# Sixteen projection blocks as two Strassen groups of 512 + 512 columns

## The chip, the cores and the metric

The kernel runs on one core of a Trainium2 chip. The metric is the time of one execution in device microseconds; the median of several runs is given. All of the big products are float32 values split in two parts, a rounded high part ("hi") and the rest ("lo"), and each product is made as three TensorE matmuls: hi x hi, lo x hi and hi x lo.

## The reference

One encoder layer on x of 512 tokens by 2048:

```
h = rmsnorm(x, norm_g)
proj = h @ w_in                      # 2048 x 10752
qa, ka, va, za, qb, kb, vb, zb, ga, gb = split(proj)
oa = diff_attention(rope(qa), rope(ka), va)      # branch A: 8 heads, two softmaxes each
ob = gqa_attention(rope2d(rmsnorm(qb)), rope2d(rmsnorm(kb)), vb)   # branch B: 8 heads, 2 of k and v
ya = (rmsnorm(oa) * silu(za)) @ w_out_a
yb = (ob * silu(zb)) @ w_out_b
x = x + (sigmoid(ga) * ya + sigmoid(gb) * yb) @ w_o
return rmsnorm(x, final_g)
```

What matters here is proj. Its columns for q, k and v are numbered in 36 blocks of 128: 0 to 7 are A's k, 8 to 15 A's q, 16 to 23 A's v, 24 and 25 B's k, 26 and 27 B's v, and 28 to 35 B's q, one block for each of B's heads.

## The kernel before

**The order of the work.** First h is made, turned and split, while blocks 0, 1, 8 and 9 are computed plainly (`stream_steps`, L137). Then the four groups of `STRASSEN_BLOCKS` (L39), four blocks each, go through `strassen` (L186) by way of `project` (L429); then twelve more Strassen groups make the gates (L476 to L488). These sixteen groups follow each other on TensorE. Then come the sixteen heads in the order of `HEADS` (L41), with "fill" work between them, then w_out_a and, in four Strassen groups, w_o.

**A Strassen group** takes 512 columns as a left and a right half of 256, the 2048 rows of weights as an upper and a lower half, and the 512 tokens as two halves. Seven products of half the size (a11, a12, s1, s2, s4, s3, a22 by the names of their activation part) take the place of eight; the weight parts are combined by subtractions on VectorE (`sub`, L207, line L209) and the products by additions (`plus`, L239, line L240, and `done`). A product is 16 x 3 matmuls of 256 columns. Its weights come from HBM in two raw tiles of 128 x 1024 into eight slots (`raw_tile`, L110); `split_w` (L113) has ScalarE write w_hi (L103) and VectorE w_lo (L104) into the pool `wp` (L82, three buffers of each). Results are added up in a PSUM bank of the ring `acc`; `share_banks` (L67) says which of the eight banks are `acc` and which `aux`, and `bank` (L69) takes the next one. A finished quarter of a group is written to the DRAM tile pv by `keep_cols` (L299), one DMA for each block, issued on SP like all DMAs.

**Plain blocks.** `FILL_BLOCKS` (L40) are eight pairs of blocks that are computed plainly as fill work. Pairs with blocks under 16 go through `plain_rows` (matmuls of 512 columns), the others through `plain_cols` (L314; natural form, matmuls of 256 columns, x as the stationary part). A pair has eight steps, each a `yield` of `stream_steps`. Behind them stand 32 steps of w_out_b and one more. `fill(n)` (L817) makes n steps. The order of TensorE's instructions among the heads is the program's own (L822): six steps, a head's `turn`, two steps, then for every head `scores` 0 and 1, the last head's `finish`, f[0] steps, `scores` 2 and 3, the next head's `turn`, f[1] steps, `turn_p`, f[2] steps, with f the three digits of `FILLS` (L46).

**Pools.** Space in SBUF is given in stacked pools. Above xa lies xs (the tiles s1 to s4, 8 KB per partition for each of h and l, 64 KB in all), above that xn during the first stage (xt with 32 KB, and some 5 KB more), and sp (six tiles of 2 KB) after it. When xs and sp close, the pools at and atc of the heads take their place; the first tiles of atc are the tables ca, sa, tc and ts, loaded at L501 to L512. wp and the PSUM pool (L64) stay open from first to last. Elsewhere the scheduler orders each engine's instructions by the program and by what is ready.

## Time and profile before

| | us |
|---|---|
| median of 3 runs | 1378.22 (1376.71 to 1378.24) |
| the profiled execution's own time | 1376.67 |
| its span, first to last instruction | 1374.9 |
| TensorE, VectorE, ScalarE, GpSimd busy | 1350.2, 1081.1, 702.9, 84.5 |

The profile is of one execution. Busy time is the union of an engine's instructions; matmuls overlap in the record, so the time of one is read from start to start or from a count in a stretch, and not from its own duration. The sixteen Strassen groups lie between 69.4 and 714.5 us, the heads between 714.5 and some 1118 us.

### The profile page before, as it was taken

The numbers are of one execution on the slowest core, as the hardware profiler recorded it, in microseconds if no ns is written. First come the engines' busy times: TensorE is split into PE (matmuls) and PEld (weight loads), VectorE is DVE, ScalarE is ACT, GpSimd is POOL, SyncE is SP. The second block draws the span as 40 slices with busy tenths as digits, with TensorE's granted clock in tenths as the row PEclk, the third lists the DMA queues.
The fourth block names the chain that finished last, engine by engine and source line by source line (L and its number), as shares of the span: only waits on it lengthen the run. The fifth ranks groups of instructions, "written<-read, shape, count | busy, mean of one in ns | idle before, by whom it ended". The sixth has DMA issues, their size and how long they took to land.

```text
span 1374.9 us, 24100 instructions
## 1 busy us (share of the span) xinstructions
PE 1350.2 (98%) x9625; PEld 1274.1 (93%) x9625; DVE 1081.1 (79%) x1400; ACT 702.9 (51%) x1110; POOL 84.5 (6%) x94
## 2 busy tenths in 40 slices
PE   6999999999999999999999999999999999999997
PEld 6999999999999999999998888888788888899997
DVE  5977787777777777777759778787898858899886
ACT  7643333444444444444446675575676753354444
POOL 1000000000000000000003201000000010004322
PEclk9999999999999999999999999999999999999999
DMA  8245434543333444333377454545575446463333
GB/s 291 77 147 161 124 116 149 154 146 113 118 121 123 148 149 143 117 122 118 123 207 220 122 154 147 153 139 162 171 221 182 130 145 202 151 245 116 97 95 123
DMA packets 201743, 204.21 MB, mean 149 GB/s; under 512 B 11280, under 2 KB 175392, under 8 KB 200992
## 3 DMA queue, kind: packets, MB, share of 16 engines
q1 hardware_dynamic: 201632, 202.69, 47.5%
q8 instruction: 75, 1.23, 0.4%
q14 instruction: 36, 0.29, 0.1%
HBM read 165.68 MB, written 32.77 MB: 144 GB/s over the span
## 4 chain that ended last, share of the span: by engine, by line
PE 90%; DVE 4%; ACT 2%; DMA 1%; issue 1%; POOL 0%; SPq 0%; DVEq 0%; POOLq 0%; ACTq 0%
PE acc L234 55%; PE acc L175 27%; PE aux L621 3%; PE aux L608 2%; PE aux L739 1%; DVE w_lo L104 1%; PE aux L664 1%; PE aux L665 1%; DVE w_raw L209 1%; DMA rows<-og 1%; DMA xt<-in_x_dram 1%; PE aux L389 0%; DMA rows<-yg 0%; ACT sq L366 0%; ACT w_hi L103 0%
## 5 line engine op out<-in xcount | busy, mean ns | idle before, releaser
L103 ACT CAST w_hi<-w_raw 128x1024 fp32r<-128x1024 f32 x351 | 368.5, 1050 | 516.8 <-PE acc L234 397.9
L104 DVE TENSOR_TENSOR w_lo<-w_raw,w_hi 128x1024 fp32r<-128x1024 f32 x351 | 431.9, 1232 | 168.7 <-ACT w_hi L103 168.2
L209 DVE TENSOR_TENSOR w_raw<-w_raw 128x1024 f32<-128x1024 f32 x160 | 200.0, 1250 | 2.4
L234 PE MATMUL acc<-a2h,w_hi 128*128 128x256 f32 x384 | 108.7, 283 | 0.0
L234 PE MATMUL acc<-a2l,w_hi 128*128 128x256 f32 x384 | 108.7, 283 | 0.0
L234 PE MATMUL acc<-a2h,w_lo 128*128 128x256 f32 x384 | 108.7, 283 | 0.0
L234 PEld LDWEIGHTS acc<-a2h,w_hi 128*128 128x128 f32 x384 | 73.7, 192 | 0.0
L234 PEld LDWEIGHTS acc<-a2l,w_hi 128*128 128x128 f32 x384 | 73.7, 192 | 0.0
L234 PEld LDWEIGHTS acc<-a2h,w_lo 128*128 128x128 f32 x384 | 73.7, 192 | 0.0
L576 DVE TENSOR_REDUCE nmax<-aux 128x1 f32<-128x512 f32 x96 | 61.0, 681 | 7.5 <-PE aux L739 4.7
L175 PE MATMUL acc<-a1h,w_hi 128*128 128x512 f32 (+1 forms) x160 | 56.6, 358 | 0.2 <-ACT a1h L393 0.2
L175 PE MATMUL acc<-a1l,w_hi 128*128 128x512 f32 (+1 forms) x160 | 55.6, 353 | 0.1
L175 PE MATMUL acc<-a1h,w_lo 128*128 128x512 f32 (+1 forms) x160 | 55.7, 353 | 0.0
L175 PE MATMUL acc<-a2l,w_hi 128*128 128x512 f32 (+1 forms) x160 | 55.5, 348 | 0.0
L175 PE MATMUL acc<-a2h,w_hi 128*128 128x512 f32 (+1 forms) x160 | 55.5, 350 | 0.0
L175 PE MATMUL acc<-a2h,w_lo 128*128 128x512 f32 (+1 forms) x160 | 55.4, 347 | 0.0
L234 PE MATMUL acc<-s4h,w_lo 128*128 128x256 f32 x192 | 54.3, 283 | 0.0
L234 PE MATMUL acc<-a1h,w_hi 128*128 128x256 f32 x192 | 54.3, 283 | 0.0
L234 PE MATMUL acc<-a1l,w_hi 128*128 128x256 f32 x192 | 54.3, 283 | 0.0
L234 PE MATMUL acc<-a1h,w_lo 128*128 128x256 f32 x192 | 54.3, 283 | 0.0
L234 PE MATMUL acc<-s1h,w_hi 128*128 128x256 f32 x192 | 54.3, 283 | 0.0
L234 PE MATMUL acc<-s1l,w_hi 128*128 128x256 f32 x192 | 54.3, 283 | 0.0
(325 smaller groups left out, 4356.0 us busy)
## 6 DMA issues: line engine op xcount, KB each, us to landing
w_raw<-in_w_in_dram SPq DMA_DIRECT2D x136, 512.0 KB, 3.6
w_raw<-in_w_in_dram SPq DMA_DIRECT2D x64, 256.0 KB, 3.7
w_raw<-in_w_o_dram SPq DMA_DIRECT2D x32, 512.0 KB, 4.4
gg<-kept SPq DMA_DIRECT2D x32, 256.0 KB, 2.4
w_raw<-in_w_out_b_dram SPq DMA_DIRECT2D x32, 256.0 KB, 3.5
rows<-gg SPq DMA_DIRECT2D x32, 256.0 KB, 3.4
w_raw<-in_w_out_a_dram SPq DMA_DIRECT2D x32, 256.0 KB, 3.4
cols<-pv SPq DMA_DIRECT2D x26, 256.0 KB, 3.3
```

Of the source, the lines that this page charges most:

```text
L103: nc.scalar.copy(out=hi, in_=src)
L104: nc.vector.tensor_tensor(out=lo, in0=src, in1=hi.bitcast(F32), op=ALU.subtract)
L175: nc.tensor.matmul(out=acc[b][:, place], lhsT=l, rhs=r, start=first and kc == order[0] and k == 0 and i == 0, stop=last and kc == order[-1 ...
L209: nc.vector.tensor_tensor(out=d, in0=u, in1=v, op=ALU.subtract)
L234: nc.tensor.matmul(out=ps[u] if by_row else ps[:, u, :], lhsT=l, rhs=r, start=n % (2 if by_row else 4) == 0 and k == 0 and i == 0, stop=n ...
L576: nc.vector.tensor_reduce(out=nmax, in_=sps, axis=AX.X, op=ALU.max, negate=True)
L608: nc.tensor.transpose(out=tp[:, i * P:(i + 1) * P], in_=self.p[i][:, j * P:(j + 1) * P], identity=ident)
L621: nc.tensor.matmul(out=o, lhsT=l, rhs=r, start=j == 0 and i == 0, stop=j == NT - 1 and i == 2)
L664: nc.tensor.matmul(out=sp, lhsT=qs[:, sl], rhs=kh, start=True, stop=False)
L665: nc.tensor.matmul(out=sp, lhsT=qs[:, sl], rhs=kl, start=False, stop=True)
L739: nc.tensor.matmul(out=sp, lhsT=l, rhs=r, start=n == 0, stop=n == 2)
```

## The change

The first Strassen group stays. Blocks 20 to 35 become two groups of the new function `strassen_wide`: 512 left and 512 right columns, the same seven products, each with 8 x 2 x 3 matmuls of 512 columns. x is the stationary part, as in the narrow groups of the projection. A product adds up in a pair of PSUM banks; for that the PSUM pool is closed and opened again as four pairs, and after the wide groups as eight banks. The raw weights of a wide group are sixteen tiles, eight in the old slots and eight in a new pool `wide`, which opens when xn and the first parts pool have closed and also holds the sums u, c and t. The parts pool is closed and opened four times: three buffers of 128 x 1024 before, four of 128 x 512 for the wide groups (a split is now made for each 128 rows of weights), three of 128 x 1024 after. In the first wide group (`late`) the right upper part is loaded before the left lower one, and s1 is made before a12. The pairs (32, 33) and (34, 35) leave `FILL_BLOCKS`, so 81 steps stand between the heads instead of 97; `FILLS` and `HEADS` are new.

```diff
--- before.py
+++ after.py
@@ -36,14 +36,16 @@
     for i in range(n)
 }
 
-STRASSEN_BLOCKS = [(16, 17, 18, 19), (20, 21, 22, 23), (24, 25, 26, 27), (28, 29, 30, 31)]
-FILL_BLOCKS = [(32, 33), (2, 10), (3, 11), (34, 35), (4, 12), (5, 13), (6, 14), (7, 15)]
-HEADS = "B0 B1 A0 B2 B3 B4 B5 A1 A2 B6 B7 A3 A4 A5 A6 A7".split()
+STRASSEN_BLOCKS = [(16, 17, 18, 19)]
+WIDE_BLOCKS = [tuple(range(20, 28)), tuple(range(28, 36))]
+FILL_BLOCKS = [(2, 10), (3, 11), (4, 12), (5, 13), (6, 14), (7, 15)]
+HEADS = "B0 B1 A0 B2 B3 B4 B5 A1 B6 B7 A2 A3 A4 A5 A6 A7".split()
 
 WIDE = "0125"
 
 FILL_FIRST = 6
-FILLS = "141 141 131 131 030 021 032 142 121 350 121 131 332 331 222 232".split()
+FILLS = "131 121 131 121 030 021 022 131 130 120 131 131 222 222 222 122".split()
 
 
 @with_exitstack
@@ -61,8 +63,13 @@
     const = ctx.enter_context(tc.tile_pool(name="const", bufs=1))
     dram = ctx.enter_context(tc.tile_pool(name="dram", bufs=1, space=bass.MemoryType.DRAM))
 
-    ps_pool = ctx.enter_context(tc.tile_pool(name="ps", bufs=1, space=bass.MemoryType.PSUM))
+    ps_pools = ctx.enter_context(ExitStack())
     banks = {}
+    def new_banks(unit):
+        ps_pools.close()
+        banks["pool"] = unit, ps_pools.enter_context(
+            tc.tile_pool(name="ps_" + unit, bufs=1, space=bass.MemoryType.PSUM))
 
     def share_banks(**kw):
         banks.update(kw)
@@ -70,7 +77,8 @@
     def bank(kind, shape):
         ring = banks[kind]
         ring.append(ring.pop(0))
-        return ps_pool.tile([P, *shape], F32, name=kind, tag=f"bank{ring[-1]}")
+        unit, pool = banks["pool"]
+        return pool.tile([P, *shape], F32, name=kind, tag=f"{unit}{ring[-1]}")
 
     def acc_tile(*shape):
         return bank("acc", shape)
@@ -79,7 +87,11 @@
         return bank("aux", shape or (S,))
 
     wraw = ctx.enter_context(tc.tile_pool(name="wraw", bufs=1))
-    wp = ctx.enter_context(tc.tile_pool(name="wp", bufs=3))
+    wp = {}
+    def parts_pool(stack, bufs=3):
+        wp["pool"] = stack.enter_context(tc.tile_pool(name="wp", bufs=bufs))
 
     ident = const.tile([P, P], F32, name="ident")
     make_identity(nc, ident)
@@ -114,8 +126,7 @@
 
         shape = list(raw.shape)
         if free is None:
-            hi = wp.tile(shape, F32R, name="w_hi", tag="w_hi")
-            lo = wp.tile(shape, F32R, name="w_lo", tag="w_lo")
+            hi, lo = (wp["pool"].tile(shape, F32R, name=n, tag=n) for n in ("w_hi", "w_lo"))
         else:
             hi, lo = (raw_tile(free + i, shape[1:], F32R) for i in range(2))
         hi_lo(hi, lo, raw)
@@ -276,6 +287,83 @@
         o = [slots[2 * i:2 * i + 2] for i in range(4)]
         slots[:] = o[1] + o[0] + o[3] + o[2]
 
+    wide_slots = list(range(16))
+    def strassen_wide(w, left, right, act, wide, done, late=False):
+        H = NK // 2
+        def load(q, half, pieces):
+            tiles = []
+            for p in range(4):
+                n = wide_slots[q * 4 + p]
+                r = raw_tile(n, (2, S)) if n < 8 else wide.tile([P, 2, S], F32, name="w_raw", tag=f"w_wide{n}")
+                row, at = (half * H + p * 2) * P, 0
+                for c0, n in pieces:
+                    nc.sync.dma_start(out=r[:, :, at:at + n],
+                                      in_=w[row:row + 2 * P, c0:c0 + n].rearrange("(k p) n -> p k n", p=P))
+                    at += n
+                tiles.append(r)
+            return tiles
+        def sub(dst, x0, x1):
+            for d, u, v in zip(dst, x0, x1):
+                nc.vector.tensor_tensor(out=d, in0=u, in1=v, op=ALU.subtract)
+        def product(name, b):
+            ps = acc_tile(2, S)
+            ah, al = act[name]
+            for kk in range(H):
+                hi, lo = split_w(b[kk // 2][:, kk % 2, :])
+                for u in range(2):
+                    sl = slice(u * P, (u + 1) * P)
+                    for i, (l, r) in enumerate(((ah, hi), (al, hi), (ah, lo))):
+                        nc.tensor.matmul(out=ps[:, u, :], lhsT=l[:, kk, sl], rhs=r,
+                                         start=kk == 0 and i == 0, stop=kk == H - 1 and i == 2)
+            return ps
+        def tmp(tag):
+            return wide.tile([P, 2, S], F32, name="wide_" + tag, tag="wide_" + tag)
+        def plus(dst, ps, sb):
+            nc.vector.tensor_tensor(out=dst, in0=ps, in1=sb, op=ALU.add)
+            return dst
+        b11, b12 = load(0, 0, left), None
+        if late:
+            b12 = load(1, 0, right)
+        b21 = load(2, 1, left)
+        b12 = b12 or load(1, 0, right)
+        b22 = load(3, 1, right)
+        p1 = product("a11", b11)
+        u = tmp("u")
+        nc.scalar.copy(out=u, in_=p1)
+        if not late:
+            p2 = product("a12", b21)
+        sub(b11, b12, b11)
+        p5 = product("s1", b11)
+        if late:
+            p2 = product("a12", b21)
+        done(0, 0, plus(tmp("c"), p2, u))
+        sub(b11, b22, b11)
+        p6 = product("s2", b11)
+        plus(u, p6, u)
+        t = plus(tmp("t"), p5, u)
+        sub(b12, b22, b12)
+        p3 = product("s3", b12)
+        plus(u, p3, u)
+        done(1, 1, plus(tmp("c"), p5, u))
+        sub(b21, b21, b11)
+        done(0, 1, plus(t, product("s4", b22), t))
+        done(1, 0, plus(u, product("a22", b21), u))
+        o = [wide_slots[4 * i:4 * i + 4] for i in range(4)]
+        wide_slots[:] = o[0] + o[3] + o[1] + o[2]
     zg = dram.tile([2 * BW, S], F32, name="zg")
     gg = dram.tile([2 * D, S], F32, name="gg")
     og = dram.tile([2 * BW, S], F32, name="og")
@@ -335,8 +423,11 @@
 
         return stream_steps(w_in, column_pieces(blocks), NK, False, act, kept, **kw)
 
+    new_banks("bank")
     share_banks(acc=[0, 1, 2, 3], aux=[4, 5, 6, 7])
     with tc.tile_pool(name="xs", bufs=1) as xs:
+        phase = ExitStack()
+        parts_pool(phase)
 
 
         for n in ("s1", "s2", "s3"):
@@ -452,7 +543,29 @@
 
             project(STRASSEN_BLOCKS[0], early, in_xt, before={"s2": late_sums})
 
+        phase.close()
+        names = dict(enumerate(slots))
+        slots[:] = [names[i] for i in (2, 3, 0, 1, 4, 5, 6, 7)]
+        new_banks("pair")
+        share_banks(acc=[0, 1, 2, 3])
+        with tc.tile_pool(name="wide", bufs=1) as wide:
+            parts_pool(phase, 4)
+            for n, blocks in enumerate(WIDE_BLOCKS):
+                def kept(th, ch, v, blocks=blocks):
+                    keep_cols(blocks[ch * 4:ch * 4 + 4], th * 2, 2, v)
+                strassen_wide(w_in, column_pieces(blocks[:4]), column_pieces(blocks[4:]), xq, wide, kept, late=n == 0)
+            phase.close()
+        o = [wide_slots[4 * i:4 * i + 4] for i in (0, 2, 1, 3)]
+        order = [slots[n] for q in o for n in q if n < 8]
+        slots[:] = order[0:2] + order[4:6] + order[2:4] + order[6:8]
         with tc.tile_pool(name="sp", bufs=6) as sp:
+            parts_pool(phase)
+            new_banks("bank")
+            share_banks(acc=[0, 1, 2, 3], aux=[4, 5, 6, 7])
             def tmp():
                 return sp.tile([P, 2, 256], F32, name="kept", tag="kept")
 
@@ -487,7 +600,9 @@
 
                     strassen(w_in, c0 + g, c0 + g + 256, xq, False, tmp, gate)
 
+            phase.close()
+    parts_pool(ctx)
     share_banks(acc=[4, 5], aux=[6, 7, 0, 1, 2, 3])
 
 

```

## Rows read from the trace of the kernel before

**Rows 1.** The page: busy time by engine, and the span in 40 slices.

```profile
PE 1350.2 (98%) x9625; PEld 1274.1 (93%) x9625; DVE 1081.1 (79%) x1400; ACT 702.9 (51%) x1110; POOL 84.5 (6%) x94
PE   6999999999999999999999999999999999999997
DVE  5977787777777777777759778787898858899886
```

**Rows 2.** The chain that ended last: start us, us, what.

```profile
69.38 645.12 PE acc L234 x5376
...
731.81 1.05 ACT w_hi L103
732.86 0.75 issue
733.61 1.20 PE aux L587 x8
734.82 7.23 PE acc L175 x48
...
1019.89 8.17 PE acc L175 x36
...
1118.96 79.37 PE acc L175 x350
```

**Rows 3.** Busy time by stretch (us, instructions): a projection group, and the heads.

```profile
69.40:109.70 40.30, 40.30 (x338) 40.30 (x338) 29.55 (x28) 16.81 (x19) 0.00 (x0) 1.00 0.46 147
742.00:1118.00 376.00, 374.50 (x1880) 315.61 (x1879) 310.99 (x574) 254.91 (x524) 23.91 (x21) 1.00 0.54 162
```

**Rows 4.** TensorE by line and form: xcount | busy us, mean ns.

```profile
L175 PE MATMUL acc<-w_hi,a2h 128*128 128x256 f32 x64 | 19.0, 298 | 0.0
...
L175 PE MATMUL acc<-w_lo,a2h 128*128 128x256 f32 x64 | 18.8, 294 | 0.0
```

**Rows 5.** VectorE and ScalarE by line and form, same columns.

```profile
L104 DVE TENSOR_TENSOR w_lo<-w_raw,w_hi 128x1024 fp32r<-128x1024 f32 x351 | 431.9, 1232 | 168.7 <-ACT w_hi L103 168.2
L209 DVE TENSOR_TENSOR w_raw<-w_raw 128x1024 f32<-128x1024 f32 x160 | 200.0, 1250 | 2.4
L240 DVE TENSOR_TENSOR kept<-acc,kept 128x512 f32<-128x512 f32 x45 | 31.1, 691 | 21.4 <-PE acc L234 20.9
L104 DVE TENSOR_TENSOR kl<-kd,kh 128x512 fp32r<-128x512 f32 x16 | 10.9, 679 | 0.4 <-ACT kh L103 0.4
L802 DVE TENSOR_TENSOR rows<-acc,rows 128x512 f32<-128x512 f32 x16 | 10.8, 684 | 1.5 <-PE acc L175 1.4
L883 DVE TENSOR_TENSOR mg<-rows 128x512 f32<-128x512 f32 x16 | 10.5, 684 | 0.1
L103 ACT CAST w_hi<-w_raw 128x1024 fp32r<-128x1024 f32 x351 | 368.5, 1050 | 516.8 <-PE acc L234 397.9 <-PE acc L175 65.9 <-issue 44.5
L103 ACT CAST kh<-kd 128x512 fp32r<-128x512 f32 x16 | 9.9, 621 | 4.6 <-PE aux L739 3.3 <-PE aux L664 0.9
```

**Rows 6.** VectorE in order of time, 98 to 122 us: start us, us, what.

```profile
106.19 2.49 DVE L209 TENSOR_TENSOR w_raw<-w_raw 128x1024 f32<-128x1024 f32 x2
...
109.73 0.69 DVE L432 TENSOR_TENSOR xt<-acc,early 128x512 f32<-128x512 f32 x1
```

**Rows 7.** SP's DMA issues in order of time, 98 to 122 us, same columns.

```profile
99.66 0.88 SPq L303 DMA_DIRECT2D pv<-xt  x2
...
104.69 6.91 SPq L303 DMA_DIRECT2D pv<-xt  x4
113.48 0.35 SPq L501 DMA_DIRECT2D ca<-in_cos_a_dram  x1
```

**Rows 8.** DMA issues: xcount, KB each, median us to landing.

```profile
pv<-kept SPq DMA_DIRECT2D x24, 128.0 KB, 1.9
pv<-xt SPq DMA_DIRECT2D x8, 128.0 KB, 2.3
```

**Rows 9.** Stretches of 1 us: PEclk is the third column from the right.

```profile
734.00:735.00 1.00, 1.00 (x10) 0.95 (x9) 1.00 (x2) 0.58 (x2) 0.66 (x1) 0.88 1.06 315
735.00:736.00 1.00, 1.00 (x6) 1.00 (x6) 1.00 (x3) 0.49 (x2) 0.00 (x0) 0.50 0.99 259
...
738.00:739.00 1.00, 1.00 (x9) 1.00 (x9) 1.00 (x3) 0.00 (x0) 0.00 (x0) 0.92 0.55 168
```

**Rows 10.** Stretches between the transposes of heads A3 to A7.

```profile
1000.40:1028.10 27.70, 27.70 (x132) 23.15 (x131) 26.65 (x46) 20.11 (x39) 0.00 (x0) 1.00 0.75 222
1028.10:1058.40 30.30, 30.30 (x144) 25.30 (x143) 26.93 (x47) 21.93 (x42) 1.30 (x1) 1.00 0.59 187
1058.40:1081.10 22.70, 22.57 (x110) 18.73 (x108) 20.16 (x37) 17.65 (x37) 1.29 (x1) 1.00 0.44 138
1081.10:1108.80 27.70, 27.66 (x129) 23.05 (x130) 24.78 (x42) 19.28 (x38) 2.27 (x2) 1.00 0.45 145
```


## The prediction

> **What bounds the kernel now.** I read the page first: TensorE is busy for 98% of the span and in nearly every slice, VectorE for 79% [rows 1]. A busy TensorE can still wait, so the chain of waits in order of time came next [rows 2]. The reader is to see that it is almost TensorE alone. The sixteen Strassen groups of the projection and the gates are one piece of 5376 products in 645.12 us, so 120.0 ns for one of 256 columns, without a hole. In the heads a block of 36 products of 512 columns takes 8.17 us, so 227 ns each. The difference of 107 ns for 256 columns leaves about 13 ns for each product whatever its width: fewer, wider products are cheaper. Third came the stretches [rows 3]: in the heads VectorE is busy 311 of 376 us, a second engine close to its limit. So TensorE's issue rate bounds the kernel, and a change is worth what it takes from TensorE's list less every new hole in that list.
>
> **The products, a gain.** Three Strassen groups (blocks 20 to 31) go: 3 x 336 x 120.0 ns = 120.96 us. Two plain pairs (32,33 and 34,35) go from between the heads: six rows of 64 products of 256 columns, 384 x 120.0 ns = 46.08 us [rows 4, 2]; their form is natural, so they too are 256 wide. In come 2 groups x 7 products x 8 x 2 x 3 = 672 matmuls of 512 columns at 227 ns = 152.5 us. Net -14.5 us. That the trace never shows the new function makes the 227 ns a transfer: the 512-wide products of w_out run 350 in 79.37 us, the same 227 [rows 2], and load as many weights per product. I keep 225 to 230 ns (2 us either way).
>
> **VectorE and ScalarE inside a wide group, nothing.** A group needs 56 splits of 512 columns, 16 subtractions of 1024 and 7 additions of 1024. An addition that reads PSUM takes as long as one in SBUF (0.69 and 0.68 for 512), so by 0.68, 1.25 and 1.25 us [rows 5] that is 67 of 76.3 us at most, and less where instructions overlap (two subtractions in 2.49 us, [rows 6]). ScalarE has 56 x 0.62 + 1.1 = 36 us. TensorE covers both; without that cover a product boundary could cost one split, 0.7 us, 13 times.
>
> **First handover (group 16 to 19 to the wide ones), a loss.** The parts buffers w_hi and w_lo used to live for the whole kernel; now their pool is closed and opened again. In KB per partition above xs: old parts 24, then xn of 37; afterwards wide takes 8 x 4 + 3 x 4 = 44 and the new parts 16, so the new parts lie at 44 to 60, inside the old xn (24 to 61). What happens to such space is in the trace: ca, which depends on nothing in the projection, is loaded at 113.48 us, just when the last results written from xt (in xn) can have landed [rows 7]. So the first wide split starts at 113.48, where TensorE ran out of products at 69.38 + 40.32 = 109.70. Add ScalarE 0.62 and VectorE 0.68 for a split of 512, less two products that need only w_hi (0.45): 3.78 + 0.62 + 0.68 - 0.45 = 4.6 us, during which nothing else is ready. In the old kernel those splits were made two halves ahead. Bounds: 0 if the space is not waited for, 5.5 with a landing 0.9 us slower than the median of 1.9 to 2.3 us that such writes have [rows 8]. I take 4.6. The wide loads behind it (b21, b22) wait for the same space, but "late" puts s1 before a12, so they have two products (22 us) to land.
>
> **The ring of PSUM pairs in the first wide group, a loss.** With "late" the order is a11, s1, a12, s2, s3, s4, a22 on pairs 0, 1, 2, 3, 0, 1, 2. So s4 wants the pair of s1, and s1's sum is last read by the addition behind s3 (u + p3, then p5 + u). Those two additions of 1024 start when s3 ends: 1.14 + 1.25 + 0.1 for semaphores = 2.5 us in which TensorE waits; the splits of a22 wait behind those of s4, so nothing overtakes. The second group has the old order and meets no such reuse. No product boundary in the trace of before shows a wait of this kind [rows 2], so the lower bound is 0; the upper is 3.6, one more subtraction in between.
> The Trainium skill (Perfetto Trace Analysis, Matmuls) asks that independent matmul groups rotate through different PSUM banks so that evacuation lies beside the next group. By that rule this order is a fault; by the row alone the sum would be 4.2 us lower. The trace of before agrees with the rule only in that its rotation shows no wait.
>
> **Second handover (wide to gates), a loss.** The new parts pool (24 KB behind 12 KB of sp) lies inside wide's 44. Its first user waits for all of wide, so for the last result u of the last group: addition 1.25, then the delay from that addition's end to freed space, 113.48 - 110.42 = 3.06 us [rows 6, 7], with four result writes instead of two, 0.44 each, so 3.94. Then a full split, 1.05 + 1.23, less two products (0.24): 7.2 us. Bounds: 0 if only the tiles beneath are waited for (the parts would lie over weight tiles, which are free early), 8.5 with slow landings. I take 7.2, nearest to the first handover's row.
> The third handover (gates to heads) costs nothing: the last parts pool lies under xs, whose last reader s4 ends one product, 5.8 us, before the gates do, and a split needs 2.3.
> The tables (ca to ts_k) are issued on SP after the wide groups instead of at 113 us; SP's next urgent load comes only after a whole product, and the heads start some 480 us later.
>
> **The clock.** The one wait of TensorE in the middle of the kernel, from 731.8 to 733.6 us [rows 2], was followed by a granted clock of 0.50, the lower of the two levels, in 735 to 738 us; the missing shares add up to 0.12 + 3 x 0.50 + 0.08 = 1.7 us [rows 9]. The 48 products behind it took 7.23 us instead of 5.76. All three new holes are longer than this one, so 3 x 1.7 = 5.1 us. Bounds: 0, and 10 if the longer ones cost double.
>
> **The heads, a loss.** 16 of 97 steps go, the 46 us above. I follow the four stretches from A3 to A7 [rows 10]: 108.4 us, VectorE 98.5, with 27 steps (the digits of FILLS). After, 22 steps: each step is 12 products, 2.73 us of TensorE, but only half a split and half a product with gg, 0.62 + 0.34 = 0.96 us of VectorE [rows 5]. TensorE would need 108.4 - 13.7 = 94.7, VectorE 98.5 - 4.8 = 93.7: 99%, in a queue that works in order. The chain of softmax then surfaces; I take 1 us for each of four of these heads, 4 us. Bounds 0 (the slack is spread well) and 12 (2 us for each A head and the B heads before them). What is late next is turn_p, which waits for the last p.
>
> **Sum.** Against the profiled execution's own 1376.67 us: -14.5 + 4.6 + 2.5 + 7.2 + 5.1 + 4.0 = +8.9, so 1385.6; that execution is 1.55 us below the median of 1378.22, so I say 1386.
>
> **Rivals.**
> (a) Not slower: the parts buffers wait at neither handover, and TensorE's gain comes through. Place: the first split of each new pool; it decides if that split starts before the previous stage's last product ends. For it: the raw weight tiles are passed on in an order that has the first ones free early. Against: the row of ca. 1376.7 - 14.5 + 2.5 + 1.7 + 4 = 1370.4.
> (b) About the same: only the tiles beneath are waited for, so the first handover stays (xt is one tile) and the second goes, with its clock: 1385.6 - 7.2 - 1.7 = 1376.7. The row of ca fits this too.
> (c) VectorE becomes the bound of the heads: the term of 4 becomes 12 to 16, so 1394 to 1398. For it: the 99%. Against: VectorE's own durations overlap in part, so 99% overstates it.
> (d) The change does not shorten TensorE's list, if 512 columns cost twice 256: 672 x 240 = 161.3 instead of 152.5, so 1394. The rows of w_out speak against it.
>
> **How the numbers follow.** Forecast 0.54 (own range 1380 to 1394), a 0.20, b 0.12, c 0.12, d 0.02. 0.2% (2.8 us) is about what a measurement of this kernel can tell from no change, so the same means 1375.5 to 1381. Slower takes c, d and 0.48 of the forecast, 0.62; the same takes the forecast's other 0.06 and 0.10 of b, 0.16; faster takes a and the last 0.02 of b, 0.22. The range of 8 in 10 runs from 1370 to 1395.
>
> **What would show it.** In the changed kernel: 672 products on one new line at 227 ns; TensorE idle 4 to 5 us near 110 us, ended by ScalarE's first w_hi, which waited for a DMA; 2.5 us near 171 us, ended by an addition on VectorE; 7 us near 273 us; a clock of 0.5 after each. Gates untouched at 40.3 us a group; heads some 42 us shorter, not 46. I am wrong if the first w_hi of the new pools is ready before the stage before has ended, or if the heads shorten by the full 46.

## The result, and the profile after

The changed kernel takes 1399.63 us in the median of four runs (1398.56 to 1401.21), the kernel before 1377.47 in four (1375.69 to 1378.24): a ratio of 1.0164, with a 95% interval of 1.0146 to 1.0181. It is slower, as forecast, but by 22 us where 8 were forecast, and outside the range. The profiled execution took 1400.52 us, 0.9 above the median; its span is 1398.7 us, 23.8 more than before.

The page of the changed kernel, its busy times and TensorE's row of the 40 slices, answers to [rows 1]:

```profile
PE 1346.0 (96%) x8905; PEld 1238.6 (89%) x8905; DVE 1099.4 (79%) x1463; ACT 717.5 (51%) x1167; POOL 86.0 (6%) x94
PE   6998999899999999999999899999998999999997
```

TensorE has 720 instructions fewer, but only 4 us less of busy time, and four slices that were full are not. The stretches say where that lies (us, then TensorE, weight load, VectorE, ScalarE and GpSimd busy, granted clock, DMA share, GB/s). Before, the fifteen groups behind the first took 40.32 us each, 604.8 in all, without a hole [rows 2, 3]; then came the heads:

```profile
714.30:1118.80 404.50, 401.16 (x2084) 341.71 (x2083) 331.64 (x614) 269.16 (x563) 33.12 (x39) 1.00 0.55 164
```

Now the two wide groups and the first handover end at 281.7, the twelve gates at 768.2 and the heads at 1143.1:

```profile
109.80:114.50 4.70, 0.22 (x3) 0.03 (x1) 0.74 (x2) 0.70 (x2) 0.00 (x0) 0.78 0.20 58
114.50:281.70 167.20, 158.02 (x673) 129.65 (x673) 124.85 (x159) 71.57 (x115) 0.00 (x0) 0.96 0.41 126
119.50:171.00 51.50, 51.50 (x228) 42.62 (x228) 43.72 (x56) 24.51 (x39) 0.00 (x0) 1.00 0.45 143
...
281.70:768.20 486.50, 486.03 (x4032) 485.74 (x4033) 369.64 (x355) 212.71 (x232) 0.00 (x0) 1.00 0.44 135
768.20:1143.10 374.90, 358.24 (x1700) 296.23 (x1699) 315.46 (x605) 257.02 (x550) 33.99 (x39) 0.99 0.53 159
```

From 109.8 us on, wide groups and gates take 171.9 + 486.5 = 658.4 us, 53.6 more than the fifteen narrow groups. The heads take 374.9, 29.6 less than before. The rest of the kernel is unchanged (255.6 us against 256.1). 53.6 - 29.6 - 0.5 is 23.5, the difference of the spans within the reading of the borders.

The third of these rows tells that the products are as cheap as forecast: 228 matmuls of 512 columns in 51.5 us, 226 ns each, with TensorE busy throughout. So the list of TensorE did get shorter, by the 14.5 us of the forecast, and some 38 us went into waits and low clock. What TensorE waited for, in us in total, times and the longest (between 60 and 1150 us; those of over a us, and one of half a us that belongs to the second handover):

```profile
PE acc L186 <- DVE w_lo L116: 6.3, 1, 6.3
PE acc L245 <- ACT w_hi L115: 6.0, 1, 6.0
PE acc L324 <- ACT w_hi L115: 4.5, 1, 4.5
PE aux L702 <- DMA cols<-pv: 4.2, 1, 4.2
PE acc L324 <- DVE wide_c L332: 3.1, 1, 3.1
PE acc L186 <- DVE rows L917: 2.0, 1, 2.0
PE aux L723 <- DVE p L788: 1.9, 3, 1.0
...
PE acc L245 <- DVE w_lo L116: 0.5, 1, 0.5
```

L324 is the product of a wide group, L245 that of a narrow one, L186 a fill step between the heads. Three of these rows are the three forecast holes: L324 on w_hi (first handover), L324 on wide_c (the PSUM pair), L245 on w_hi (second handover, with the half us on w_lo right behind it). The timelines of SP, ScalarE and VectorE (start us, us, what) show each at its place:

```profile
110.75 1.16 SPq L391 DMA_DIRECT2D pv<-xt  x2
...
113.80 2.18 ACT L115 CAST w_hi<-w_raw 128x512 fp32r<-128x512 f32 x4 [11.48 <-DMA pv<-xt]
...
171.45 1.23 DVE L332 TENSOR_TENSOR wide_u<-acc,wide_u 128x1024 f32<-128x1024 f32 x1 [0.24 <-PE acc L324]
172.59 0.68 DVE L116 TENSOR_TENSOR w_lo<-w_raw,w_hi 128x512 fp32r<-128x512 f32 x1
173.18 1.22 DVE L332 TENSOR_TENSOR wide_c<-acc,wide_u 128x1024 f32<-128x1024 f32 x1
...
276.93 1.95 SPq L391 DMA_DIRECT2D pv<-wide_u  x4
...
280.58 2.94 ACT L115 CAST w_hi<-w_raw 128x1024 fp32r<-128x1024 f32 x3 [9.95 <-DMA pv<-wide_u]
```

At 113.8 us ScalarE splits the first wide tile and was released by the result writes from xt, as [rows 7] let one expect from ca. At 280.6 it was released by the writes from u, issued at 276.93, so 3.65 us earlier. Between them, at 171.45, stand the two additions that free the pair of s4, and between the two a split that the forecast had not seen in VectorE's queue. Behind each of the three holes the granted clock was 0.50, the lower level. The stretches in which TensorE worked at it, and two in the heads:

```profile
114.50:119.50 5.00, 5.00 (x12) 3.91 (x13) 5.00 (x7) 2.10 (x4) 0.00 (x0) 0.52 0.95 322
...
174.50:181.00 6.50, 6.45 (x16) 5.08 (x17) 1.39 (x2) 1.23 (x2) 0.00 (x0) 0.52 0.52 158
...
281.70:287.00 5.30, 4.83 (x22) 4.54 (x23) 3.68 (x4) 1.82 (x2) 0.00 (x0) 0.54 0.35 116
...
788.80:791.70 2.90, 2.83 (x11) 2.66 (x12) 2.90 (x7) 1.17 (x2) 1.12 (x1) 0.50 0.98 251
...
1085.00:1089.00 4.00, 4.00 (x10) 3.18 (x11) 2.82 (x3) 0.00 (x0) 0.00 (x0) 0.54 0.61 198
```

The missing shares of the first three add up to 2.4 + 3.1 + 2.4 = 7.9 us. With the waits of 4.5, 3.1, 6.0 and 0.5 us, that is 22.0 of the 53.6; the other 31.5 is the products' own longer list there (152.5 - 120.96). The last two stretches belong to the heads, whose waits are the other half of the story: in the list above those of L186, L702 and L723, with smaller ones (0.9 us on pl, 0.6 each on og1h and og1l), come to 16.5 us, against 3.2 before, of which the 1.8 at the start stands in [rows 2].

The heads A3 to A7 answer to [rows 10], between the same transposes; here the third of the four stretches, and all four together (us and the same columns):

```profile
1075.50:1109.70 34.20, 27.23 (x120) 22.11 (x119) 26.95 (x44) 19.95 (x41) 1.26 (x1) 0.90 0.47 146
...
1027.20:1132.70 105.50, 97.27 (x450) 80.03 (x448) 93.18 (x165) 74.90 (x152) 5.15 (x4) 0.97 0.50 153
```

VectorE has 93.2 us of work in them (93.7 forecast), but they take 105.5 us where the forecast had 94.7 + 4. The third stretch has most of the difference: TensorE stood there for 7 of 34.2 us. This is the wait of 6.3 us, in the timelines of ScalarE, VectorE and TensorE:

```profile
1076.38 1.03 ACT L115 CAST w_hi<-w_raw 128x1024 fp32r<-128x1024 f32 x1
...
1077.44 1.29 DVE L917 TENSOR_TENSOR rows<-acc,rows 128x512 f32<-128x512 f32 x2
...
1082.90 2.05 DVE L116 TENSOR_TENSOR w_lo<-w_raw,w_hi 128x1024 fp32r<-128x1024 f32 x1
...
1085.01 0.80 PE L186 MATMUL acc<-og1h,w_lo 128*128 128x512 f32 x1 [6.31 <-DVE w_lo L116]
```

The high part of the weights is ready at 1077.4. Its low part is made only from 1082.9 on: two products of rows (the fill steps' own), four pl and three y (the heads') stand before it in VectorE's queue, 5.5 us. A fill step that is there to cover the head waits mostly for the heads' own VectorE work.

### The profile page after: what moved, and what is told of

Its sections match the earlier page's. It is cut to its first block, busy times and chain, and to the rows that moved or that the text cites. A ratio compares the mean times of both kernels' runs of the same rounds, so it can differ in the third digit from the quotient of the medians.

```text
span 1398.7 us, 22873 instructions
## 1 busy us (share of the span) xinstructions
PE 1346.0 (96%) x8905; PEld 1238.6 (89%) x8905; DVE 1099.4 (79%) x1463; ACT 717.5 (51%) x1167; POOL 86.0 (6%) x94
## 5 line engine op out<-in xcount | busy, mean ns | idle before, releaser
L115 ACT CAST w_hi<-w_raw 128x1024 fp32r<-128x1024 f32 (+1 forms) x413 | 385.1, 934 | 531.4 <-PE acc L245 318.1
L116 DVE TENSOR_TENSOR w_lo<-w_raw,w_hi 128x1024 fp32r<-128x1024 f32 (+1 forms) x413 | 446.8, 1089 | 171.8 <-ACT w_hi L115 171.3
L220 DVE TENSOR_TENSOR w_raw<-w_raw 128x1024 f32<-128x1024 f32 x136 | 170.7, 1256 | 1.9
L245 PE MATMUL acc<-a2h,w_hi 128*128 128x256 f32 x384 | 108.7, 283 | 0.0
L245 PE MATMUL acc<-a2l,w_hi 128*128 128x256 f32 x384 | 108.7, 283 | 0.0
L245 PE MATMUL acc<-a2h,w_lo 128*128 128x256 f32 x384 | 108.7, 283 | 0.0
L245 PEld LDWEIGHTS acc<-a2h,w_hi 128*128 128x128 f32 x384 | 73.7, 192 | 0.0
L245 PEld LDWEIGHTS acc<-a2l,w_hi 128*128 128x128 f32 x384 | 73.7, 192 | 0.0
L245 PEld LDWEIGHTS acc<-a2h,w_lo 128*128 128x128 f32 x384 | 73.7, 192 | 0.0
L245 PE MATMUL acc<-a1h,w_hi 128*128 128x256 f32 x192 | 55.3, 288 | 6.0 <-ACT w_hi L115 6.0
L186 PE MATMUL acc<-og1h,w_lo 128*128 128x512 f32 x128 | 50.8, 396 | 6.3 <-DVE w_lo L116 6.3
L186 PE MATMUL acc<-a1h,w_hi 128*128 128x512 f32 (+1 forms) x160 | 56.3, 357 | 0.2 <-ACT a1h L484 0.2
L186 PE MATMUL acc<-a2h,w_hi 128*128 128x512 f32 (+1 forms) x160 | 56.1, 354 | 0.0
L245 PE MATMUL acc<-a1h,w_lo 128*128 128x256 f32 x192 | 55.3, 288 | 0.5 <-DVE w_lo L116 0.5
L186 PE MATMUL acc<-a2l,w_hi 128*128 128x512 f32 (+1 forms) x160 | 55.7, 349 | 0.0
L186 PE MATMUL acc<-a2h,w_lo 128*128 128x512 f32 (+1 forms) x160 | 55.7, 349 | 0.0
L186 PE MATMUL acc<-a1h,w_lo 128*128 128x512 f32 (+1 forms) x160 | 55.5, 351 | 0.0
L186 PE MATMUL acc<-a1l,w_hi 128*128 128x512 f32 (+1 forms) x160 | 55.2, 350 | 0.1
L245 PE MATMUL acc<-a1l,w_hi 128*128 128x256 f32 x192 | 55.1, 287 | 0.0
L245 PE MATMUL acc<-s1h,w_hi 128*128 128x256 f32 x192 | 54.3, 283 | 0.0
L245 PE MATMUL acc<-s1l,w_hi 128*128 128x256 f32 x192 | 54.3, 283 | 0.0
```

The costliest lines, as they stand in the source:

```text
L115: nc.scalar.copy(out=hi, in_=src)
L116: nc.vector.tensor_tensor(out=lo, in0=src, in1=hi.bitcast(F32), op=ALU.subtract)
L186: nc.tensor.matmul(out=acc[b][:, place], lhsT=l, rhs=r, start=first and kc == order[0] and k == 0 and i == 0, stop=last and kc == order[-1 ...
L220: nc.vector.tensor_tensor(out=d, in0=u, in1=v, op=ALU.subtract)
L245: nc.tensor.matmul(out=ps[u] if by_row else ps[:, u, :], lhsT=l, rhs=r, start=n % (2 if by_row else 4) == 0 and k == 0 and i == 0, stop=n ...
```

## The experiments

The kernel before, run beside each batch of them, had medians of 1375.1 to 1376.9 us, against 1377.5 beside the changed kernel. Ratios are to the kernel before of the same batch; a difference of medians from the changed kernel is good to some 2 us only, so the stages of the profiled executions stand beside it.

**The three holes one by one.** In e1_ring the two next pairs of the ring change places before s4 of the first wide group, so that s4 gets a pair that has been free for long.

```diff
+        if late:
+            r = banks["acc"]
+            r[0], r[1] = r[1], r[0]
         done(0, 1, plus(t, product("s4", b22), t))
```

> The first wide group takes its last two PSUM pairs in the other order, so that s4 gets the pair of a12 and a22 that of s1. Theory (TensorE waited for the pair of s1): the hole of 3.6 us near 171 us goes and the low clock behind it too (some 3.1 us), so about 6.7 us less than the changed kernel, near 1393 us. Rival (VectorE is simply behind at that boundary, with the splits of s4 late): a hole of 2 us or more stays near 171 us and the time falls by under 3 us.

Measured: 1394.58 us, 1.0142 of the kernel before (1.0120 to 1.0164), 5.0 less than the changed kernel by the medians and 6.2 by the spans. Its gates end at 762.2 us instead of 768.2, 6.0 earlier. Its list of TensorE's waits has the two handovers as they were and no row on wide_c:

```profile
PE acc L245 <- ACT w_hi L115: 6.0, 1, 6.0
PE acc L324 <- ACT w_hi L115: 4.5, 1, 4.5
```

So the order of products against the ring makes this hole, and its price is the wait (3.1 us) and the low clock behind it (3.1). The Trainium skill (Perfetto Trace Analysis, Matmuls) asks that independent groups rotate through different PSUM banks; the 6.0 us agree.

In e2_u_apart the sum u lies in a pool of its own, above the parts, so that what is written last from the wide groups is not in the space that the gates' parts take.

```diff
-            return wide.tile([P, 2, S], F32, name="wide_" + tag, tag="wide_" + tag)
+            return (up if tag == "u" else wide).tile([P, 2, S], F32, name="wide_" + tag, tag="wide_" + tag)
...
             parts_pool(phase, 4)
+            up = phase.enter_context(tc.tile_pool(name="up", bufs=1))
```

> The sum u lives in a pool of its own above the parts buffers, so that the space the gates' parts buffers come to lie in no longer waits for the last result's write to memory. Theory (the second handover waits for that write): the hole of 7 us near 275 us shrinks to the 1.3 us of the last addition (the PSUM pool is still handed over), without a low clock behind it: 7.0 + 2.4 - 1.3 = 8 us less than the changed kernel, near 1391.5 us. Rival (the PSUM handover or the first gate group's weights decide): a hole of over 4 us stays.

Measured: 1393.68 us, 1.0132 (1.0115 to 1.0149), 5.9 less. The wait of 6.0 us on w_hi is gone; what is late next is the addition itself:

```profile
PE acc L245 <- DVE wide_u L332: 1.7, 1, 1.7
```

So the second handover is the wait for u's result write, and rival (b), by which it costs nothing, falls; whether the space waits for the whole pool, or only because the new parts come to lie over u, this run does not tell. The gain is 2 us short of the 8 expected. In the profiled executions the gates end 7.7 us earlier (760.5 instead of 768.2), of which 1.5 is a shorter low clock behind the ring's hole (last section), and the heads, where nothing was changed, take 1.5 us longer.

In e3_parts_low the wide groups' parts pool is opened before `wide`, so it takes another part of the freed space, and closes after it.

```diff
+        parts_pool(phase, 4)
         with tc.tile_pool(name="wide", bufs=1) as wide:
-            parts_pool(phase, 4)
...
-            phase.close()
+        phase.close()
```

> The wide groups' parts pool opens before the pool wide, so it lies where the old parts were and no longer over xt. Theory (the first handover waits for the write of the last results out of xt): the hole of 5 us near 110 us shrinks to about 1 us, one split of 512, and the low clock behind it goes: 6.5 us less than the changed kernel, near 1393 us. The other two holes stay. Rival (the PSUM pool or the wide weights decide): a hole of over 3 us stays near 110 us.

Measured: 1398.45 us, 1.0159 (1.0143 to 1.0174), 1.2 less, which is no difference, and a miss. The first hole did shrink, but the second grew. Its waits:

```profile
PE acc L245 <- ACT w_hi L115: 7.8, 1, 7.8
...
PE acc L324 <- DVE xt L523: 0.9, 1, 0.9
```

SP's issues ahead of the gates, in order of time, and the gates' first split on ScalarE:

```profile
269.94 1.96 SPq L391 DMA_DIRECT2D pv<-wide_u  x4
271.95 0.48 SPq L580 DMA_DIRECT2D lam<-in_lambda_k_dram  x1
...
275.22 1.99 ACT L115 CAST w_hi<-w_raw 128x1024 fp32r<-128x1024 f32 x2 [11.70 <-DMA lam<-in_lambda_k_dram]
```

The space was handed on in another order. The result writes from u go out as soon after the last addition as before, but the last of four small loads (lam) now stands right behind them on SP, and by the trace it is this load that releases the gates' first split, 1.8 us later than the writes did. That the first hole comes from where the parts lie is shown (4.5 to 0.9 us). With the low clock behind it, its going is worth 6 us, and the gates do end 5.4 earlier (762.8 instead of 768.2), for the low clock behind the ring's hole was shorter this time. The heads give 3.3 us of it back, though nothing in them was changed and their waits add up to 17.0 us, against 16.5:

```profile
762.80:1141.00 378.20, 361.20 (x1701) 298.33 (x1700) 315.94 (x605) 257.01 (x550) 33.55 (x39) 0.98 0.53 158
```

TensorE is busy there for 361.2 us instead of 358.2 with the same work, at a mean clock of 0.98 instead of 0.99: nearly the same waits were followed by more low clock (last section).

e5_all_three has the three edits together, with u's pool opened right above `wide`.

> The three edits to the wide part together: the other order of the PSUM pairs, the parts pool below the pool wide, and the sum u in a pool above wide. Theory (the wide part's loss is these three holes and the low clock behind them): holes of about 1 us near 110 us and 2 to 3 us near 263 us are left, none near 165 us, no or one short stretch of low clock; the changed kernel's 57 us for handovers and wide groups over the narrow groups' list shrinks to some 36 us, so 16 to 18 us less than the changed kernel, near 1382 us, and the heads stay as they are. Rival (holes only move, as one did when the parts pool alone was moved): under 12 us less, over 1387 us.

Measured: 1381.95 us, 1.0044 (1.0027 to 1.0061), 17.7 less than the changed kernel, as expected. The profiled execution took 1386.59, some 4.6 us more than the other three. Its wide groups, gates and heads:

```profile
109.80:265.00 155.20, 153.01 (x675) 126.10 (x673) 125.04 (x160) 72.45 (x116) 0.00 (x0) 1.00 0.44 134
265.00:751.30 486.30, 485.63 (x4033) 485.46 (x4034) 369.57 (x355) 212.55 (x232) 0.00 (x0) 1.00 0.44 136
751.30:1129.20 377.90, 361.26 (x1700) 298.36 (x1700) 315.91 (x605) 256.60 (x550) 33.40 (x39) 0.98 0.53 158
```

The wide groups now take 155.2 us instead of 171.9, at full clock. The holes' price was 14.1 us of waits (4.5, 3.1, 6.5) and 7.9 of clock; the repair leaves waits of 0.9, 1.4 and 0.6 us. The heads of this execution are 3.0 us longer than the changed kernel's, again with waits of 16.5 us and more low clock; that the three shorter executions lack this is not shown, but their mean granted clock was 0.993 and 0.994, and 0.990 here. The 6 us that are left over the kernel before are the heads' 16.5 and these small waits with their clock, against the 14.5 of the products.

**The heads alone.** e4_five_narrow is the kernel before with a fifth narrow Strassen group of blocks 32 to 35 and the changed kernel's fill blocks, digits and order of heads: no wide group, no new pool.

```diff
-STRASSEN_BLOCKS = [(16, 17, 18, 19), (20, 21, 22, 23), (24, 25, 26, 27), (28, 29, 30, 31)]
-FILL_BLOCKS = [(32, 33), (2, 10), (3, 11), (34, 35), (4, 12), (5, 13), (6, 14), (7, 15)]
+STRASSEN_BLOCKS = [(16, 17, 18, 19), (20, 21, 22, 23), (24, 25, 26, 27), (28, 29, 30, 31),
+                   (32, 33, 34, 35)]
+FILL_BLOCKS = [(2, 10), (3, 11), (4, 12), (5, 13), (6, 14), (7, 15)]
```

> The kernel of before with blocks 32 to 35 as a fifth narrow Strassen group and the new lists of fills and heads; nothing is wide. TensorE's list alone says 40.3 - 46.1 = 5.8 us less than before, near 1372 us. Theory (the heads lose some 15 us of the 46 us because VectorE fills up and one wait at their start grows): 40.3 - 31 = 9 us more than before, near 1387 us, with the heads at 373 us as in the changed kernel. Rival (the heads' loss comes from the wide part, by late tables or another order of DMAs): the heads shorten by 42 us or more and the time is 1372 to 1376 us.

Measured: 1386.84 us, 1.0077 (1.0062 to 1.0092). TensorE has one group of 40.32 us more and 46.08 us of fill work less, and the kernel is still 11.7 us slower. The stretch of its heads:

```profile
754.80:1128.80 374.00, 358.16 (x1701) 296.30 (x1700) 316.69 (x606) 258.34 (x551) 33.49 (x39) 0.99 0.53 160
```

And the longest of its waits:

```profile
PE acc L176 <- DVE w_lo L105: 6.3, 1, 6.3
```

374.0 us, and the same wait of 6.3 us: the loss of the heads has nothing to do with the wide groups. It comes with the steps that were taken out, or with the new digits and the new order of heads, which came with them and were not tried by themselves.

e12_one_wide turns this round: one wide group (blocks 20 to 27) with the repairs of e5, two narrow groups, and the kernel before's fill work, digits and order of heads.

> One wide group alone (blocks 20 to 27), with the three edits to the wide part; blocks 28 to 31 stay a narrow Strassen group, 32 to 35 stay plain, and the lists of fills and heads are those of before. So the heads are untouched. Theory: two narrow groups of 40.3 us become one wide one of 76.3, 4.3 us less, and the two handovers that are left cost 1.0 + 2.3 us and up to 1.7 of low clock: within 0.2% of before (1374 to 1378 us on the chip where before has 1376), with the heads at 404 us as before. Rival (the heads' loss also comes from what the wide part does to the order of loads): the heads get longer by 3 us or more and the time lies over 1379 us.

Measured: 1379.19 us in eight runs against 1375.65 in twelve, 1.0027 (1.0016 to 1.0038), a little over the 1374 to 1378 expected. Its wide group, and its heads:

```profile
110.80:188.70 77.90, 76.56 (x336) 62.89 (x336) 61.86 (x80) 35.89 (x58) 0.00 (x0) 1.00 0.41 132
...
715.30:1120.00 404.70, 400.87 (x2084) 341.79 (x2083) 330.27 (x613) 267.94 (x562) 32.37 (x39) 1.00 0.55 164
```

With the old fill work the heads take 404.7 us, as before (404.5). The wide group takes 77.9 us where two narrow ones took 80.6; the waits at its borders (0.9, 1.4 and 0.6 us) and a low clock behind them eat that gain and a little more. The profile is of the fastest of the eight executions (1376.94), so it does not show where the rest of the 3.5 us lies.

**What in the heads is short.** e7_no_rope leaves out the rotation of branch A's q and k, three VectorE operations of 0.68 us for each, so that VectorE has less to do.

```diff
-        nc.vector.tensor_tensor(out=o, in0=o, in1=sa, op=ALU.mult)
-        nc.vector.tensor_tensor(out=v, in0=v, in1=ca, op=ALU.mult)
-        nc.vector.tensor_tensor(out=v, in0=v, in1=o, op=ALU.add)
```

> The rotation of branch A's queries and keys is left out (three VectorE operations of 512 columns for each of 16 blocks, 29 us of VectorE's time); loads and TensorE's list stay. Theory (VectorE's queue holds TensorE in the heads): the waits between 980 and 1110 us mostly go, the one of 6.6 us above all, and the heads shorten by 8 to 13 us, so 1387 to 1392 us. Rival (latency of the chain from scores to transposes, or transfers): the waits stay where they are, under 3 us less.

Measured: 1392.18 us, 1.0116 (1.0101 to 1.0132), 7.4 less than the changed kernel; the heads of the profiled execution are 8.1 shorter (366.8 us instead of 374.9), at the lower end of the 8 to 13 expected. The transposes of A3 and A7 in TensorE's timeline:

```profile
1029.00 1.25 PE L720 MATMUL aux<-ident,p 128*128 128x128 f32 x10
...
1125.12 1.91 PE L720 MATMUL aux<-ident,p 128*128 128x128 f32 x16
```

And its longest wait between 1000 and 1110 us:

```profile
PE acc L186 <- DVE rows L914: 2.2, 1, 2.2
```

A3 to A7 takes 96.1 us instead of 105.5, and the wait on w_lo is gone. So VectorE's work in this run of heads sets their time; 96.1 is also near the 94.7 us that the forecast gave TensorE there. In all the heads, TensorE's waits fall from 16.5 us to 8.2, so half of them are left.

**Repairs of the heads.** None worked, and each tells how tight the order is. e6_fills moves three steps from early heads (B0, B5, B6) to A4, A5 and A6, where the long wait is.

```diff
-FILLS = "131 121 131 121 030 021 022 131 130 120 131 131 222 222 222 122".split()
+FILLS = "121 121 131 121 030 021 021 131 120 120 131 131 232 232 232 122".split()
```

> Three of the 73 steps between the heads move from B0, B5 and B6 to A4, A5 and A6 (their middle digit 2 becomes 3); everything else is the changed kernel's. Theory (VectorE's queue is full in the run of A heads, while the B heads have room): the B intervals shorten by 2.7 us each without a new wait, and the waits of TensorE between A3 and A6 (2.1, 1.1, 0.8 and 6.6 us, and the low clock behind) lose about half: 4 to 8 us less than the changed kernel. Rival (a head's own chain of softmax sets the waits, so each step taken from a B head uncovers as much): no change within 2 us.

Measured: 1402.1 us, 1.0193 (1.0178 to 1.0208), no faster than the changed kernel, a miss. The wait on w_lo is gone, but new ones have come at 985 to 1005 us:

```profile
PE acc L186 <- ACT og1h L115: 8.1, 3, 3.5
```

Branch B's results are split for w_out_b in the fill steps themselves (`og_split`). With fewer steps early on, the first of these splits comes 10.6 us before the matmul that needs it (981.4 and 992.0 us), where the changed kernel has 16.4 (971.3 and 987.7), and the later ones come too late. e8_all_fills has these digits on top of e5's repairs:

> The three edits to the wide part and the moved steps together. Theory: the two gains add, 20 to 26 us less than the changed kernel, 1374 to 1380 us, about the kernel of before. Rival (the gain of the moved steps depends on when the heads start, or does not exist): as the three edits alone, near 1382 us.

Measured: 1384.23 us, 1.0062 (1.0047 to 1.0077): nothing gained on e5, a miss.

e9_rope_pool is e5 with the rotation on GpSimd, which is nearly idle in the heads (busy for 33 of 378 us in e5).

> The three edits to the wide part, and branch A's rotation (three operations for each of 16 blocks) on GpSimd instead of VectorE; all of the computation is there. Theory (VectorE's queue holds TensorE among the A heads, and a block's rotation has two heads' time): the waits of 6.6, 1.0 and 0.8 us between 1035 and 1096 us go as they did where the rotation was left out, 5 to 8 us less than the three edits alone (1382), near 1376 us. Rival (GpSimd and VectorE hold each other up, so VectorE's own operations get longer): under 3 us less, with VectorE's mean times up by 5% or more in that stretch.

Measured: 1387.36 us, 1.0083 (1.0063 to 1.0103), 5 slower than e5, a miss. The wait on w_lo goes and others come. Its longest new wait:

```profile
PE acc L186 <- DVE rows L920: 4.1, 1, 4.1
```

And the rotation's first operation, in the groups of instructions (count, us busy, mean ns, idle before):

```profile
L664 POOL TENSOR_TENSOR other<-other,sa 128x512 f32<-128x512 f32 x16 | 24.1, 1508 | 39.5 <-DMA other<-pv 32.8 <-DVE nmax L694 6.5
```

An operation of 0.68 us on VectorE takes 1.5 us there, and VectorE itself gets slower beside it (last section).

e10_first7 is e5 with seven steps instead of six before the first turn, and one instead of two behind it, for the wait of 4.2 us on cols.

```diff
-FILL_FIRST = 6
+FILL_FIRST = 7
...
-        fill(2)
+        fill(1)
```

> The three edits to the wide part, and seven instead of six steps ahead of the first head's turn, one instead of two behind it. Theory (the wait of 4.7 us at the heads' start is for the first head's blocks to be loaded and prepared, and a step of 2.7 us is its cover): that wait falls to about 2 us and nothing new appears behind the turn: 2.7 to 5 us less than the three edits alone, near 1378 us. Rival (the step behind the turn covered the split of the turned q): the wait moves there, within 1 us of 1382.

Measured: 1386.18 us, 1.0073 (1.0055 to 1.0092), 4 slower than e5, a miss. The wait at the start falls to 1.8 us, but one of 3.3 us on ql appears behind it. e11_both joins e9 and e10:

> Both edits to the heads with the three to the wide part. Theory: the gains add to 8 to 12 us, 1370 to 1374 us, under the kernel of before. Rival: the later or shifted heads meet other waits and the sum is under 5 us, over 1377 us.

Measured: 1389.12 us, 1.0092 (1.0074 to 1.0110), a miss too. No version beat the kernel before.

## Why the prediction was right and wrong

**Right: the products.** 226 ns for 512 columns, so -14.5 us on TensorE's list. Rival (d) falls. VectorE inside a wide group cost nothing: TensorE is busy throughout from 119.5 to 171 us.

**Right: the two handovers.** The first was put at 4.6 us and the wait measured 4.5; e3 shows its cause. The second was put at 7.2 and measured 6.5 (6.0, and 0.5 on w_lo); e2 shows its cause. Rival (a) falls with them. The third handover cost nothing at the border of gates and heads, as forecast: TensorE was busy for 486.0 of the gates' 486.5 us, and the half us is the second handover's.

**Nearly right: the ring.** 2.5 forecast, 3.1 measured. The chain was right, and the split of 0.6 us between the two additions was missing from it.

**A term too small: the clock.** 5.1 forecast, 7.9 measured. The price of 1.7 us was read from one wait of 1.8 us; the longer holes cost 2.4 to 3.1 each. This lies inside the bounds that were given (0 to 10).

**The step that failed: the heads.** "I take 1 us for each of four of these heads, 4 us." The heads became 29.6 us shorter instead of 46.08, so the term was 16.5. In it are 13.3 us more waits (16.5 less 3.2) and 1.6 more of low clock (1.4 at 789 to 792 us and 1.8 at 1085 to 1089, less the 1.7 of before); the remaining 1.6 stand in no row. 16.5 us is about the price of rival (c), 12 to 16, and e4 shows it without any of the wide part (374.0 us against 404.5). But VectorE was not the bound that (c) names: from A3 to A7 it was busy 93.2 of 105.5 us. The amounts of work were right (93.2 us of VectorE against 93.7). Wrong was to take an average over four heads as the measure of a queue. VectorE took its work in the order of its queue: w_lo could have been made from 1077.4 us on and was made from 1082.9. A fill step's w_lo stands wherever the program put it, behind what the head has asked for, and one such place cost 6.3 us and 1.8 of clock behind it, twice what was put down for all heads together. The wait that was named as next, turn_p's for p, came to 1.9. e7 shows that the long one is VectorE's work: without the rotation it goes and A3 to A7 shrinks by 9.4 us. The start of the heads cost 2.4 us more than before (4.2 against 1.8), of which the forecast had nothing; the six steps ahead of the first turn are shorter now (12 x 227 ns = 2.73 us each instead of 24 x 120.0 ns = 2.88), which makes 0.9 us of it. The other waits, on rows, og1h, og1l and p, were not tried singly, so why they came stays open.

**The sum.** With the measured terms: -14.5 + 4.5 + 3.1 + 6.5 + 7.9 + 16.5 = +24.0, against 23.8 in the spans. The forecast's +8.9 lacked 12.5 in the heads and 2.8 in the clock; the three holes together were put 0.2 too high.

**The range** reached to 1395. Rival (c) was worked out with the heads alone, to 1398; its 16 together with the clock's upper bound of 10 would have given 1386 + 12 + 4.9 = 1402.9, beyond the result.

## What to carry to other kernels

Taking fill work away from between latency-bound chains can bring less than its TensorE time (here 29.6 of 46.1 us): count what every remaining step waits for in the in-order queue of its helper engine, head by head, and not the average share. When a pool of SBUF is closed and another opened in its place, the new one's first buffer can wait for the last reader of that space, result writes by DMA included (e2, e3); put the tile that is read last outside of what the next stage takes first. After reordering products, walk the PSUM ring once more, and expect a repaired wait to come up again at the next place (e3, e6, e10).

## What the runs showed of the hardware

**The low clock lasted unequally.** Behind the wait of 1.8 us before, the clock was 0.50 for 3.4 us [rows 9]. In the changed kernel it lasted 4.8 to 6.2 us behind the three holes (the missing shares above, by 0.50). The same ring hole of 3.1 us was followed in e2 by half as much, and then by the full clock from 178.30:

```profile
175.20:178.30 3.10, 3.10 (x7) 2.45 (x8) 0.00 (x0) 0.59 (x1) 0.00 (x0) 0.50 0.96 296
```

The wait of 2.0 us on rows is the same in the changed kernel (1022.5 to 1024.4 us) and in e5 (1006.9 to 1008.9). The next 4 or 5 us of work, first in the changed kernel, then in e5:

```profile
1024.00:1028.00 4.00, 3.57 (x19) 3.03 (x20) 3.97 (x7) 1.04 (x3) 0.00 (x0) 1.00 0.93 281
...
1009.10:1014.00 4.90, 4.90 (x19) 3.88 (x19) 3.98 (x6) 0.34 (x2) 0.76 (x1) 0.65 0.85 261
```

Here it cost nothing, there (1 - 0.65) x 4.9 = 1.7 us. So the price of a hole is not read from its length, and it differs between executions with the same waits; that is most of why the heads of e3 and e5 are some 3 us longer than the changed kernel's. The holes named here cost between nothing and 3.1 us of clock.

**VectorE stood while GpSimd worked.** The w_lo that TensorE waited for at 1082.90 took 2.05 us; the next one of the same form, at 1085.47, took 1.21. Over the first of the two lies this GpSimd multiplication:

```profile
1082.61 1.26 POOL L815 TENSOR_TENSOR rows<-y,rows 128x512 f32<-128x512 f32 x1 [24.88 <-DVE y L814]
```

It ends at 1083.87, and 1.2 us from there is 1085.07, against 1084.95 in the trace: as if VectorE had hardly begun before. The Trainium skill (SBUF — State Buffer, SBUF: two separate sides) says that the two engines share a pair of ports, which a VectorE instruction with two inputs in SBUF needs too, and that the one that starts first holds it for its whole instruction; this row agrees. Beside five other such multiplications in the changed kernel VectorE's pl, which reads one of its two inputs from PSUM, kept its 0.68 to 0.69 us. In e9, with 48 more such operations on GpSimd, one p of VectorE took 1.80 us where the median is 0.75, and the mean rose from 749 to 849 ns.
